# Dense steps of an input projection in runs of four, and a sum over values in one piece, in the interleaving of a decoder step

## The chip, the cores and the metric

The kernel runs on one core of one Trainium2 chip. The metric is the device time of a run in microseconds (us). The kernel before takes 839.37 us, the median of 3 runs (834.9 to 840.41).

## The reference

One step of a hybrid decoder layer, for a prompt of 512 tokens and for 8 sample sequences of 8 new tokens each behind 1024 past ones. Both groups go through the same weights, so the kernel treats them as 576 columns (T).

```python
h = _rmsnorm(x, norm1_w)
proj = h @ w_in                                   # 1024 -> 3584 columns, 28 tiles of 128
rq, rk, rv, rg, aq, ak, av = jnp.split(proj, points, axis=-1)
ro, ret_s = _retention(rq, rk, rv, ret_s0)        # 8 heads of 64, chunks of 128
ro = silu(rg) * group_norm(ro)
k_all = concat([win_k, ak]);  v_all = concat([win_v, av])
ao = _dilated_attention(aq, q_pos, k_all, v_all)  # 8 heads, softmax over three dilated windows
x = x + concat([ro, ao]) @ w_out
ua, ub = jnp.split(_rmsnorm(x, norm2_w) @ w_up, [D_FF])
x = x + (silu(causal_conv3(ua)) * ub) @ w_down    # D_FF = 2816
return _rmsnorm(x, normf_w), ...                  # and states, windows, conv rows
```

## The kernel before, in words

**Dense products.** The projections run in float32 exactness by splits: a weight tile (wraw, 128 x 1024) is split into whi (ACT, line 219) and wlo (DVE, line 229), the activations into a hi and a lo part as well. One *dense step* of k (line 254, in `dense`) is three passes (hi hi, lo hi, hi lo) over two halves of 288 columns, so six matmuls. A tile of 128 output columns takes 8 steps and sums into one of two big PSUM tiles (psd, the tile d). The weights come over SP's queue of DMAs in order of use.

**Two kinds of attention.** The heads go in four pairs (hp 0 to 3). Per pair the prompt has four *units* of 128 queries (`attn_unit`): a split of q (ACT, DVE line 755), scores (PE, 761 to 766), minimum (DVE, 773), exponential (ACT, 780), reciprocal (DVE, 783), scaling of the weights (POOL, 785), transposes (PE, 791), copies (ACT and DVE, 795), sums over values (PE, 804), and after the fourth a copy (ACT, 809). The sample group has two *units* per pair (`unit`), each of four sequences with 768 rows of the cache: per sequence two sets of three key transposes (PE, 877; six matmuls each in the trace since both sets stand together) with copies to kt (DVE and ACT, 878), then scores (PE, 887), minimum (DVE, 894), exponential (ACT, 899), reciprocal and scaling (DVE, 901 and 902), weight transposes (PE, 910 and 911), copies to spt (DVE and ACT, 914 to 916), sums over values (PE, 923; 28 groups), a copy ob (ACT, 932), its transpose (PE, 938) and the copies into aoT (DVE, 941). The cache tiles (kc, three buffers; vc, six) are loaded by SP ahead of their use. POOL copies the queries of a pair into a zero-padded tile (qb), one of which the sample scores need.

**Behind the products.** The 28 column tiles of the input projection (`in_proj`) each end in a scaling on DVE (526, 528), transposes of v and k to token order (PE, 495), or the gate (tile roT: SiLU on ACT, product on POOL, for the last pair on DVE, line 532). The tiles for attention of pair hp wait until six units of pair hp-2 are used. `mix_split` splits the attention and gate results (1009 and 1011) for the output projection, which is the next dense stage. Ahead of that stage SP issues the loads of the last norm's weights (nfw, 1285) and of the convolution state (csn, 1051); PE transposes csn in 22 tiny matmuls (1055).

**What sets the order.** Nothing is scheduled on the chip: each engine's queue is written at build time by `Merge` (lines 96 to 142). A *stream* is a generator that issues some instructions and yields (cost, latency): what its burst holds TensorE for, and how long the other engines then need before the stream's next burst can start. Streams with an amount of work left (the dense products of in_proj, and the parents of attention) advance in proportion to it; a stream without goes first as soon as it is ready. A dense step yields a cost of 738 ns. A stream that lacks something (a PSUM tile: four small ones, m, and the two big ones; a tile of another stream) yields None. Retention ends at `mg.run(lambda: fin_ret)`; from there to the output projection the streams are in_proj, the prompt units and the sample units.

```python
            ok = [e for e in free if e["at"] <= self.clock]
            if ok:
                e = min(ok, key=lambda e: (e["left"] is not None, e["vt"] if e["left"] else e["at"], e["n"]))
            else:
                e = min(free, key=lambda e: (e["at"], e["n"]))
                self.clock = e["at"]
```

Of the kernel before, what the change touches and what calls it, by code (L numbers as in the profile page):

```python
# [35 lines left out]
C0 = 224  # L36
# [59 lines left out]
class Merge:  # L96
    """Interleaves streams of tensor-engine work.

    A stream is a generator; it yields (cost, latency): what its last burst holds the tensor engine for,
    and how long the other engines then take before its next burst can start.  A third number, if given,  # L100
    takes the place of the cost in the pace.  None: it waits for another stream.  Streams with work
    left advance in proportion to it; a stream without goes first as soon as it is ready."""

    def __init__(self):
        self.clock, self.live, self.n = 0.0, [], 0

# [3 lines left out]
    def add(self, gen, left=None, delay=0.0):  # L110
        self.n += 1
        self.live.append({"g": gen, "left": left, "vt": self.floor(), "at": self.clock + delay, "n": self.n,
                          "stuck": False})

    def run(self, until=None):
        while self.live and not (until and until()):
# [3 lines left out]
            if ok:  # L120
# [9 lines left out]
            if c is None:  # L130
                e["stuck"] = True
                continue
            low = self.floor()
# [13 lines left out]
def decoder_step(ctx, tc, a):  # L147
# [14 lines left out]
    def room(n):  # L162
        """n of the small tiles of PSUM are free from here on; give() returns them when their readers are issued"""
# [13 lines left out]
    # ---- weights, streamed in order of use  # L177
# [67 lines left out]
    def dense(ps, key, xhi, xlo, k0, k1, first, last, rows=None, made=None):  # L245
        """ps[:, C0 + n] (+)= sum over k of w[k, cols]^T x[k, n], in three exact-split passes."""
# [19 lines left out]
    # ---- constants  # L266
# [31 lines left out]
    def rsqrt_steps(dst, v, t):  # L298
        """dst = v ** -0.5 for positive v: a seed from the exponent, then Newton's steps; t: scratch."""
# [24 lines left out]
    # ================= first norm  # L324
# [114 lines left out]
    def in_first():  # L439
        """the first two tiles of columns advance together as x arrives"""  # L440
# [34 lines left out]
    # ================= input projection, retention and dilated attention, by pairs of heads  # L475
# [13 lines left out]
    def natural(src, dst):  # L489
        """dst [token, tile, 128] = the transpose of src [128 features, T]"""  # L490
# [101 lines left out]
    # ---- retention  # L592
# [12 lines left out]
    def retention():  # L605
        for hp in range(4):
# [13 lines left out]
            # scores, transposed: [key, query]  # L620
# [19 lines left out]
            # states after each chunk  # L640
# [13 lines left out]
            # outputs  # L654
# [21 lines left out]
            # group norm; the decay of a row only scales its statistics  # L676
# [29 lines left out]
            # states of the sample group  # L706
# [616 lines left out]
```

## Time and profile before

| | before |
|---|---|
| median of 3 runs | 839.37 us (834.9 to 840.41) |
| profiled execution, span | 838.0 us, one execution |
| TensorE (PE) busy | 817.6 us, 98% |
| VectorE (DVE) busy | 414.1 us, 49% |
| ScalarE (ACT) busy | 295.2 us, 35% |
| GpSimd (POOL) busy | 148.4 us, 18% |
| from the end of retention to the output projection | 148.46 to 338.39 us of the span |
| DMA, mean over the span | 154 GB/s |

The profile is of one execution on the chip. PE is TensorE's matmuls, PEld its weight loads, SPq the queue of SyncE that issues DMAs; PEclk is the granted clock of TensorE as a share of full speed (1.00 is 2.4 GHz, 0.5 is 1.2 GHz). A row of a timeline names start, duration, engine, line, operation, out<-in with shapes, how many instructions it stands for, and in brackets the idle time ahead of it and what ended it. Matmuls are pipelined, so a row's duration overlaps the next; the distance from start to start is what a group costs.

### The profile page before, as it was taken

To read this page: it belongs to the slowest core of one execution; us is meant where nothing else is said; L and a number is where in the kernel's file an instruction comes from. 1 tells how busy PE (TensorE), PEld (TensorE's weight loads), DVE (VectorE), ACT (ScalarE), POOL (GpSimd) and SP (SyncE) were. 2 spreads that over 40 slices of the span, in tenths; PEclk is the share of its full clock that TensorE was granted. 3 is DMA by queue.
4 is the path that set the end of the run, shared out by engine and by line. 5 is a ranking of instruction groups with operands and counts; after the bars stand their busy time and mean duration, and the time that the engine had idled before them with its cause. 6 is when DMAs were issued, how large, how long until landed. Compare 5 with 4: busy or idle time off the path is not lost.

```text
span 838.0 us, 16048 instructions
## 1 busy us (share of the span) xinstructions
PE 817.6 (98%) x6594; PEld 775.0 (92%) x6594; DVE 414.1 (49%) x796; ACT 295.2 (35%) x511; POOL 148.4 (18%) x234
## 2 busy tenths in 40 slices
PE   7999999998999999999999999999999999999995
PEld 6999999886887888999999999999999999999995
DVE  5664655655556456544555455432235545545333
ACT  5322321544536367234223333311223323332222
POOL 1312111020111113022212222100012222210111
PEclk9999999999999999899999999999999999999999
DMA  9355562667796873555256544453334445553213
GB/s 268 104 167 163 162 201 70 184 187 217 201 251 184 237 201 85 109 176 169 84 179 198 176 158 138 135 170 87 94 101 156 146 152 176 170 169 81 70 51 114
DMA packets 179534, 128.68 MB, mean 154 GB/s; under 512 B 15425, under 2 KB 176101, under 8 KB 178914
## 3 DMA queue, kind: packets, MB, share of 16 engines
q1 hardware_dynamic: 178308, 93.75, 40.1%
q10 hardware_dynamic: 928, 33.63, 11.0%
q8 instruction: 52, 0.85, 0.4%
q0 software_dynamic: 224, 0.28, 0.1%
q14 instruction: 22, 0.18, 0.1%
HBM read 121.52 MB, written 39.66 MB: 192 GB/s over the span
## 4 chain that ended last, share of the span: by engine, by line
PE 92%; DMA 3%; DVE 1%; ACT 1%; SPq 1%; issue 1%; POOL 0%; ACTq 0%; DVEq 0%; POOLq 0%
PE d L254 72%; PE m L877 2%; PE d L451 2%; PE m L923 2%; DMA kc<-in_cache_win_k_dram 1%; PE m L791 1%; PE d L887 1%; PE m L495 1%; PE m L804 1%; PE px L410 1%; PE m L1213 1%; PE px L254 1%; DMA csn<-in_state_conv_dram 1%; PE m L663 1%; PE m L764 1%
## 5 line engine op out<-in xcount | busy, mean ns | idle before, releaser
L219 ACT ACTIVATE whi<-wraw 128x1024 fp32r<-128x1024 f32 (+2 forms) x114 | 110.8, 972 | 372.2 <-issue 182.1
L229 DVE TENSOR_TENSOR wlo<-wraw,whi 128x1024 fp32r<-128x1024 f32 (+2 forms) x114 | 126.8, 1112 | 119.8 <-ACT whi L219 116.8
L254 PE MATMUL d<-bhi,whi 128*128 128x288 f32 x768 | 174.6, 309 | 0.0
L254 PE MATMUL d<-bhi,wlo 128*128 128x288 f32 x768 | 165.0, 297 | 0.0
L254 PE MATMUL d<-blo,whi 128*128 128x288 f32 x768 | 164.8, 296 | 0.0
L254 PE MATMUL d<-hhi,whi 128*128 128x288 f32 x704 | 150.9, 296 | 0.0
L254 PE MATMUL d<-hlo,whi 128*128 128x288 f32 x704 | 150.8, 296 | 0.0
L254 PE MATMUL d<-hhi,wlo 128*128 128x288 f32 x704 | 150.7, 296 | 0.0
L254 PEld LDWEIGHTS d<-bhi,whi 128*128 128x128 f32 x768 | 122.4, 191 | 5.3 <-issue 3.6
L254 PEld LDWEIGHTS d<-bhi,wlo 128*128 128x128 f32 x768 | 124.1, 189 | 0.0
L254 PEld LDWEIGHTS d<-blo,whi 128*128 128x128 f32 x768 | 124.1, 190 | 0.0
L254 PEld LDWEIGHTS d<-hhi,whi 128*128 128x128 f32 x704 | 113.4, 189 | 0.1
L254 PEld LDWEIGHTS d<-hhi,wlo 128*128 128x128 f32 x704 | 113.4, 189 | 0.0
L254 PEld LDWEIGHTS d<-hlo,whi 128*128 128x128 f32 x704 | 113.4, 189 | 0.0
L1122 DVE TENSOR_TENSOR ue<-d,rstd_b 128x512 f32<-128x512 f32 x22 | 15.2, 691 | 74.5 <-PE d L254 74.5
L1141 POOL TENSOR_TENSOR g<-g,cv 128x512 f32<-128x512 f32 x20 | 25.8, 1290 | 142.5 <-DVE g L1138 137.1
L785 POOL TENSOR_SCALAR s<-s,sc 128x128 f32<-128x128 f32 (+3 forms) x32 | 18.2, 578 | 141.7 <-DVE sc L783 140.4
L1038 POOL TENSOR_TENSOR acc<-acc,sq 128x576 f32<-128x576 f32 x13 | 21.4, 1646 | 111.5 <-ACT sq L1037 111.5
L1127 POOL COPY cout<-ue 128x2 f32<-128x2 f32 x22 | 5.7, 259 | 137.6 <-DVE ue L1122 137.6
L877 PE MATMUL m<-ident,kc 128*128 128x128 f32 x192 | 27.5, 277 | 2.1 <-DMA kc<-in_cache_win_k_dram 2.1
L878 DVE COPY kt<-m 128x384 f32<-128x384 f32 x32 | 17.8, 556 | 23.2 <-PE m L877 22.6
L878 ACT COPY kt<-m 128x384 f32<-128x384 f32 x32 | 15.3, 477 | 38.5 <-PE m L877 38.0
(261 smaller groups left out, 1033.7 us busy)
## 6 DMA issues: line engine op xcount, KB each, us to landing
wraw<-in_w_up_dram SPq DMA_DIRECT2D x44, 512.0 KB
wraw<-in_w_in_dram SPq DMA_DIRECT2D x26, 512.0 KB
kc<-in_cache_win_k_dram SPq DMA_DIRECT2D x32, 256.0 KB
vc<-in_cache_win_v_dram SPq DMA_DIRECT2D x32, 256.0 KB
wraw<-in_w_down_dram SPq DMA_DIRECT2D x16, 384.0 KB
wraw<-in_w_down_dram SPq DMA_DIRECT2D x16, 320.0 KB
kc<-in_cache_win_k_dram SPq DMA_DIRECT2D x64, 64.0 KB
vc<-in_cache_win_v_dram SPq DMA_DIRECT2D x64, 64.0 KB
```

The source lines that it names most:

```text
L219: act.activation(split[i][0][:, c], raw[i][:, c], AF.Copy)
L229: dve.tensor_sub(lo[:, c], raw[i][:, c], f32(hi[:, c]))
L254: pe.matmul(ps[:, C0 + s * H2:C0 + (s + 1) * H2], wt[:, rows[k] if rows else k - k0], x[k][:, s * H2:(s + 1) * H2], start=first and k == k ...
L410: pe.transpose(ps[:, s], xn[:r, j, k * P:(k + 1) * P], ident[:r, :r])
L451: pe.matmul(ps[i][:, C0 + s * H2:C0 + (s + 1) * H2], wt[:, k], x[k][:, s * H2:(s + 1) * H2], start=k == 0 and wt is hi and x is xhis, stop ...
L785: pool.tensor_scalar(s[:, :n], s[:, :n], c[:, 2:3], 1.0, op0=OP.mult, op1=OP.mult)
L877: pe.transpose(ps[:, j * P:(j + 1) * P], K[u, x][:, 3 * w + j], ident)
L878: (act.copy if w else dve.tensor_copy)(kt[:, w * 384:w * 384 + 384], ps[:, :384])
L923: pe.matmul(ps[x * 32:(x + 1) * 32, :P], pt[:n, j, x * 32:(x + 1) * 32], v, start=j == 0, stop=j == 6, tile_position=(0, x * 32))
L1038: pool.tensor_tensor(acc, acc, sq, op=OP.add)
L1122: dve.tensor_mul(u[:, 2:NP + 2], ya[:, :NP], rstd_b[:, :NP])
L1141: eng.tensor_tensor(g[:, :NP], g[:, :NP], c[:, :NP], op=OP.mult)
```

## The change

`Merge` gets a number `keep` (1, as before, or 4) and remembers which stream ran last and how many bursts in a row it has run. A stream that was added as dense, that ran last and is still ready goes on until it has run `keep` bursts. Only in_proj is added as dense; keep is 4 from the end of retention to the end of `mix_split`. In the sample unit the sums over values no longer hand back after the fourth of seven row blocks. Comments and docstrings also went, so that a line of before stands 8 lines further on after it in the functions named above (L254 is L262, L923 is L931).

```diff
     def __init__(self):
         self.clock, self.live, self.n = 0.0, [], 0
+        self.keep, self.burst, self.last = 1, 0, None
...
-    def add(self, gen, left=None, delay=0.0):
+    def add(self, gen, left=None, delay=0.0, dense=False):
...
             ok = [e for e in free if e["at"] <= self.clock]
-            if ok:
+            if self.last in ok and self.burst < self.keep:
+                e = self.last
+            elif ok:
                 e = min(ok, key=lambda e: (e["left"] is not None, e["vt"] if e["left"] else e["at"], e["n"]))
...
             if c is None:
                 e["stuck"] = True
+                if e is self.last:
+                    self.last = None
                 continue
+            self.burst = self.burst + 1 if e is self.last else 1
+            self.last = e if e["dense"] and c[0] and e in self.live else None
...
                     pe.matmul(ps[x * 32:(x + 1) * 32, :P], pt[:n, j, x * 32:(x + 1) * 32], v, start=j == 0, stop=j == 6,
                               tile_position=(0, x * 32))
-                if j == 3:
-                    yield 900.0, 0.0
             for x in range(4):
                 del V[u, x]
-            yield 800.0, 600.0
+            yield 1700.0, 600.0
...
-    mg.add(in_proj(), 130.0e3)
+    mg.add(in_proj(), 130.0e3, dense=True)
...
     mg.run(lambda: fin_ret)
     rpx.close()
+    mg.keep = 4
...
     mg.add(mix_split())
     mg.run()
+    mg.keep = 1
```

What this does to the order of the queues stands at three places. First TensorE in the middle of the stage, around the transpose of the first sample unit's result (tile ob; qa and ql are the splits of q of a prompt unit, s its weights, n the values of a pair in token order). Before, from the sums over values on:

```order
L923 MATMUL m<-vc,spt 32x128 x8
L923 MATMUL m<-n_1727,spt 32x128 x4
L764 MATMUL m<-kdec,qa_2061 128x512
L764 MATMUL m<-ka_1767,qa_2062 128x512
L766 MATMUL m<-kdec,ql 128x512
L766 MATMUL m<-ka_1767,ql 128x512
L254 MATMUL d<-bhi,whi 128x288 x2
L254 MATMUL d<-blo,whi 128x288 x2
L254 MATMUL d<-bhi,wlo 128x288 x2
L877 MATMUL m<-ident,kc 128x128 x6
L938 MATMUL m<-ident,ob 128x128
L254 MATMUL d<-bhi,whi 128x288 x2
```

And now, from the same scores of 512 columns on:

```order
L774 MATMUL m<-kdec,ql 128x512
L774 MATMUL m<-ka_1810,ql 128x512
L812 MATMUL m<-pt,n_1747 64x128 x6
L944 MATMUL m<-ident,ob 128x128
L885 MATMUL m<-ident,kc 128x128 x6
L769 MATMUL m<-t_1807,t_1952 128x128 x2
L895 MATMUL d<-kt,qb_404 32x512 x4
L895 MATMUL d<-kt,qb_404 32x264 x4
L799 MATMUL m<-ident,s 128x128 x10
L885 MATMUL m<-ident,kc 128x128 x6
L812 MATMUL m<-pt,n_2127 64x128 x2
L812 MATMUL m<-pt,n_1747 64x128 x8
```

The dense steps that stood between the scores, the transposes and the scores of the next unit are gone from here; the next of them comes behind the second sample unit's sums over values.

Second, TensorE at the end of the stage, from the last unit but one on. Before:

```order
L791 MATMUL m<-ident,s 128x128 x8
L923 MATMUL m<-vc,spt 32x128 x24
L923 MATMUL m<-n_3797,spt 32x128 x4
L254 MATMUL d<-bhi,whi 128x288 x2
L254 MATMUL d<-blo,whi 128x288 x2
L254 MATMUL d<-bhi,wlo 128x288 x2
L804 MATMUL m<-pt,n_3797 64x128 x8
L254 MATMUL d<-bhi,whi 128x288 x2
```

Now the dense steps of the input projection are all done ahead of this:

```order
L799 MATMUL m<-ident,s 128x128 x8
L931 MATMUL m<-vc,spt 32x128 x24
L931 MATMUL m<-n_3689,spt 32x128 x4
L812 MATMUL m<-pt,n_3689 64x128 x8
L885 MATMUL m<-ident,kc 128x128 x6
L944 MATMUL m<-ident,ob 128x128
L895 MATMUL d<-kt,qb_406 32x512 x4
L895 MATMUL d<-kt,qb_406 32x264 x4
L918 MATMUL d<-ident,ss 128x128 x6
L919 MATMUL d<-ident,ss 64x128
L931 MATMUL m<-vc,spt 32x128 x24
L931 MATMUL m<-n_3689,spt 32x128 x4
```

The last sample unit's scores, weight transposes and sums follow each other, where dense steps stood between all of them.

Third, VectorE at the same end, around the split of q (ql) for the last prompt unit. Before, with a scaling of the input projection (t) and a split of weights (wlo) ahead of it:

```order
L894 ISA ss,ssc<-d,sb 128x776
L894 ISA ssc 128x1
L526 TENSOR_TENSOR t_4173<-d,rstd_b 128x576
L795 COPY pt<-m 128x384
L229 TENSOR_TENSOR wlo<-wraw,whi 128x1024
L755 TENSOR_TENSOR ql<-t_3590,qa_4157 64x128
L755 TENSOR_TENSOR ql<-t_3590,qa_4158 64x128
```

And now, with the reciprocals of the unit before it (sc) ahead, and the last gate product (roT) behind:

```order
L886 COPY kt<-m 128x384
L902 ISA ss,ssc<-d,sb 128x776
L902 ISA ssc 128x1
L791 RECIPROCAL sc<-sc 128x1 x2
L763 TENSOR_TENSOR ql<-t_3466,qa_4148 64x128
L763 TENSOR_TENSOR ql<-t_3466,qa_4149 64x128
L540 TENSOR_TENSOR roT<-roT,t_4105 128x576
L781 ISA s,sc<-m,pb 128x512
```

The split of q now stands behind reciprocals, which come after exponentials on ACT; and the product of the last gate tile, which was the last work of the stage on VectorE, stands before the last prompt unit's minimum.

## Rows read from the trace of the kernel before

**Rows 1.** The page, part 1: busy us, share of the span, instructions.

```profile
PE 817.6 (98%) x6594; PEld 775.0 (92%) x6594; DVE 414.1 (49%) x796; ACT 295.2 (35%) x511; POOL 148.4 (18%) x234
```

**Rows 2.** Windows: start:end, length, busy (instructions) of each engine, clock, DMA share, GB/s.

```profile
148.46:338.39 189.93, 185.52 (x1815) 156.23 (x1815) 109.31 (x281) 102.80 (x247) 29.86 (x73) 1.00 0.69 193
192.85:202.42 9.57, 7.20 (x95) 5.37 (x93) 5.30 (x14) 4.96 (x14) 0.89 (x4) 1.00 0.88 250
338.39:347.34 8.95, 8.95 (x68) 8.72 (x66) 7.67 (x11) 4.17 (x6) 0.47 (x2) 1.00 0.50 97
347.34:350.98 3.64, 2.15 (x24) 2.11 (x23) 0.00 (x0) 0.00 (x0) 0.00 (x0) 0.77 1.20 252
350.98:356.30 5.32, 5.32 (x23) 5.32 (x23) 1.33 (x2) 0.00 (x0) 0.00 (x0) 0.52 0.39 95
```

**Rows 3.** Timeline of PE, the stretch without dense steps.

```profile
192.85 0.82 PE L877 MATMUL m<-ident,kc 128*128 128x128 f32 x6
...
196.13 0.89 PE L877 MATMUL m<-ident,kc 128*128 128x128 f32 x6 [1.15 <-DMA kc<-in_cache_win_k_dram]
197.40 1.00 PE L761 MATMUL m<-t,t 64*128 64x128 f32 x4 [0.39 <-DVE kt L878]
198.33 1.52 PE L923 MATMUL m<-vc,spt 128*32 128x128 f32 x48
...
200.13 1.10 PE L877 MATMUL m<-ident,kc 128*128 128x128 f32 x6
201.95 0.71 PE L791 MATMUL m<-ident,s 128*128 128x128 f32 x2 [0.72 <-POOL s L785]
```

**Rows 4.** Timeline of PE, just before that stretch.

```profile
187.25 1.51 PE L887 MATMUL d<-kt,qb 128*32 128x512 f32 x16
188.69 1.09 PE L804 MATMUL m<-pt,n 128*64 128x128 f32 x16
189.72 0.53 PE L254 MATMUL d<-bhi,whi 128*128 128x288 f32 x2
...
190.61 0.82 PE L877 MATMUL m<-ident,kc 128*128 128x128 f32 x6
191.19 0.51 PE L254 MATMUL d<-bhi,whi 128*128 128x288 f32 x2
...
192.06 0.43 PE L254 MATMUL d<-bhi,whi 128*128 128x288 f32 x2
```

**Rows 5.** Groups by line and form, end of retention to output projection: busy, mean ns | idle before.

```profile
L780 ACT ACTIVATE s<-s,sc 128x512 f32<-128x512 f32 x8 | 5.7, 714 | 1.0 <-DVE sc L773 0.9
L785 POOL TENSOR_SCALAR s<-s,sc 128x512 f32<-128x512 f32 x8 | 5.5, 697 | 30.4 <-DVE sc L783 30.4
L780 ACT ACT_TABLE_LOAD x2 | 2.6, 1283 | 0.0
```

**Rows 6.** Timeline of DVE and of ACT, one sample unit from minimum to scaling.

```profile
188.91 0.97 DVE L894 CUSTOM_DVE_ANT_0 ss<-d,sb 128x776 f32<-128x776 f32 x1 [1.65 <-PE d L887]
190.32 0.95 ACT L899 ACTIVATE ss<-ss,ssc 128x776 f32<-128x776 f32 x1
191.62 0.16 DVE L901 RECIPROCAL ssc<-ssc 128x1 f32<-128x1 f32 x1
191.81 0.62 DVE L902 TENSOR_SCALAR ss<-ss,ssc 128x776 f32<-128x776 f32 x1
```

**Rows 7.** SP from 300 to 352 us: a wait (total, times, longest), and an issue.

```profile
SPq L1285 <- DVE roT L532: 20.8, 1, 20.8
...
342.44 0.38 SPq L1051 DMA_DIRECT2D csn<-in_state_conv_dram  x1
```

**Rows 8.** Timeline of PE where the conv state arrives, in the output projection.

```profile
348.84 2.21 PE L1055 MATMUL m<-ident,csn 16*128 16x16 f32 x22 [1.50 <-DMA csn<-in_state_conv_dram]
...
351.62 0.68 PE L254 MATMUL d<-blo,whi 128*128 128x288 f32 x2
352.10 0.68 PE L254 MATMUL d<-bhi,wlo 128*128 128x288 f32 x2
```

## What the change does to the time: the prediction

> **What bounds the kernel now.** I read the page first, then the windows of the stretch that the change reorders, then its timeline on TensorE, then the waits. The page has TensorE (PE) busy for 98% of the span [rows 1], so a microsecond is won or lost where PE stands still or turns slowly. The change acts from the end of retention, at 148.5 us of the span, to the first step of the output projection, at 338.4 us. In those 189.93 us PE is busy for 185.52 [rows 2]: 4.4 us of gaps, all clock at 1.00. This stage mixes two kinds of work. Dense steps (six matmuls, all on weights that are there) can run at any time. Attention groups come in chains: scores on PE, minimum on DVE, exponential on ACT, reciprocal on DVE, scaling on POOL or DVE, transposes on PE, copies on ACT and DVE, sums over values on PE. Each group waits for other engines, and the dense steps between them are what hides the waits. So the reader should look for the one place where before has no dense steps: from 192.85 to 202.42 [rows 3]. There the queue waits 1.15 us for a cache tile, 0.39 for a copy and 0.72 for POOL. Windows give 7.20 us busy of 9.57 there [rows 2].
>
> **The change, part by part.** *Fewer switches.* The order has 118 dense steps in this stretch before and after, in 67 runs before and 29 after. A step that follows other work takes 0.87 us (191.19 to 192.06) or 0.89 (189.72 to 190.61); one that follows a dense step takes 0.79 (192.06 to 192.85) [rows 3, 4]. So 38 entries fewer at 0.08 to 0.10 each: 3.0 to 3.8, taken as **-3.2 us**. The one-piece sum over values removes no matmul; only three of the eight units were cut in before's order, and its gain is inside the 38.
>
> *Waits that lose their cover.* The kept dense stream spends its steps early. It may not run more than two pairs of heads ahead (its tile of hp waits until the units of hp-2 are used), and it ends before attention does. The new order has three stretches without a dense step: the first from the scores of pair 0's third prompt unit on, with two whole sample units in it; the second when pair 1 ends and pair 2 begins; the third at the end, up to the output projection. I added their PE groups at their quickest turns, start to next start (six key transposes 0.58, a unit's sample scores 1.44, its value sums 1.80, the largest prompt value sums 1.03 [rows 3, 4], the other kinds between 0.1 and 1.1 likewise): 21.0, 13.8 and 17.1 us, 51.9 in all. In before only the stretch of [rows 3] has this form.
>
> How long PE waits in them I worked out twice. *By the yardstick:* the dense-free stretch of before has 2.37 us idle per 7.20 busy, 0.33; but groups in it also wait inside (a set of key transposes takes 1.27 from 196.13 to 197.40, not 0.58), and at quickest turns its work is 5.6 of 9.57, so 0.71. On 51.9 us that is **17 to 37 us**. *By walking the queues* of the after order with durations of the trace:
> First stretch, 9.6 us. Transposes of weights and keys wait for small PSUM tiles whose copies stand behind score minima on DVE and copies on ACT: 2.6. Scores of the last prompt unit and the next pair, same cause: 1.2. The second sample unit's scores need the new keys that POOL copies in; POOL stands before them at two 512-wide scalings (0.70 each) that wait for two exponentials (0.71 each) [rows 5]: 2.2. The next 256-wide scores need a split of q on DVE, behind the sample unit's scaling (0.62 [rows 6]): 1.5. Its transposes come 2.1 before their chain is done.
> Second stretch, 5.8 us: 3.0 for the first unit of pair 2, whose chain minimum, exponential, reciprocal, scaling has only sample scores and one set of transposes to hide it; 0.95 for a copy of sums that stands on ACT behind key copies; 1.9 for small ones.
> Third stretch, 11.6 us. The split of q for the last prompt unit stands on DVE behind reciprocals, these wait for 384-wide exponentials, and those on ACT behind four casts and a table load of 1.28 us [rows 5]: PE is done with the groups ahead at about 5 us and gets the split at 9.5: 4.7. Transposes and value sums of the unit before it: 1.9. The last sample unit has nothing beside it at all: from the end of its scores (188.69 in the unit shown) come the minimum 0.97, exponential 0.95, reciprocal 0.16 and scaling 0.62 [rows 4, 6], 2.7 us and four hand-overs, 3.2 in all; then 0.65 for the copies ahead of its value sums, 0.45 for the one behind them; 0.7 for small ones.
> Together **+27 us**, in the middle of the yardstick's bounds. The walk has no contention in it, the upper end has; the lower end counts gaps alone. I keep 17 and 37 for the range. Against it, the 4.4 us of gaps of before go away or are counted in the walk: **-4.4**.
>
> *Behind the stage.* The load of the conv state (csn) is third in a row of waits on SP: the norm weights ahead of it wait 20.8 us for the product of the last gate tile [rows 7]. In before this tile is the last work of the stage; csn lands at 348.84, PE waits 1.5 us for it after the first 11 steps of the output projection, and behind that gap and 22 tiny transposes the clock is at 0.50, 1.2 GHz: pairs of matmuls at 0.48 us (351.62 to 352.10) instead of 0.27 [rows 2, 8]. That is 11 pairs, 5.32 us instead of 2.9. After the change the gate tile ends some 20 us ahead of the output projection, csn waits only for the last value sums, and the same 11 dense steps (8.8 us) cover it; in before it took 6.4 us from issue (342.44 [rows 7]) to landing. Gain 1.5 + 2.4 = **-3.9 us**, zero if csn is late or the clock falls all the same.
>
> Moved on SP and DVE: the cache loads keep their order; in the dense-free stretches they are asked for faster. Before moves 193 GB/s over the stage and 250 in its dense-free stretch [rows 2]; a set of key and value tiles is 0.77 MB, 3.1 us at that rate, and the second stretch wants six in 19 us with three loaded ahead: 9 us, covered. Cost nothing; if the cover is gone, some 3 us per late set. Splits of weights on ACT and DVE come in pairs ahead of a run of four steps (3.2 us); one split of each fits. Nothing.
>
> *Clock.* At 195 to 202 us PE stood for 1.15, 0.39 and 0.72 us and the windows keep 1.00 [rows 2, 3]; after the 1.5 us and the tiny transposes at 347 it fell [rows 2, 8]. The new waits are 2 to 5 us long. I put nothing into the sum, 2.4 us per fall into the range. The Trainium skill (TensorE: Matmul & The Clock Gate, Why this matters for your kernels) says that idle gaps between bursts of matmuls put the clock back to half; that would make the three stretches cost about 7 us more, and the rows at 347 agree with it, those at 195 show gaps that were too short.
>
> **Sum.** -3.2 - 4.4 + 27 - 3.9 = +15.5. The profiled span of 838.0 becomes 853.5; the median of the runs is 1.4 above the span, so **855 us**.
>
> **Rivals.** *All covered, faster.* If the chains run as well without dense steps as with them, the three stretches keep only the 4.4 us that before has, and what stays is 3.2 + 3.9: 832 us, or 828 if those 4.4 go as well. For it: DVE is busy for 109 and ACT for 103 of the 190 us, so neither is full. Against it: [rows 3], where the same chains without dense steps left PE waiting for a third to two thirds of its work. The point from which it decides: below 11.5 us of waits the change gains.
> *Short waits, no change.* The walk may overrate queues: 12 to 20 us of waits give 840 to 848. For it: small latencies that I took in line can overlap.
> *Clock falls or cache tiles late, slower still.* Half clock behind each stretch, or a late set of tiles in two of them: 7 us more, 862; with the upper yardstick 868 and above. For it: two waits of the third stretch are each longer than the one at 347. Against it: most gaps stand between full groups of matmuls.
> That the change does not do what it says is no rival: the order shows the runs of four.
>
> **How the numbers follow.** Forecast, 20 to 37 us of waits and no fall, 848 to 865: 0.52. Short waits, 840 to 848: 0.22. Clock or tiles, 860 to 875: 0.12. All covered, 829 to 838: 0.14. A measurement can tell about 1% here, 8.4 us: slower than 847.8 is the first and the third, 0.64; within 1% the second and 0.06 of the last, 0.28; faster than 831, 0.08. The range from 840 (12 us of waits) to 868 (37 us and one fall) leaves out 0.14 below and 0.05 above.
>
> **What would show it.** Right: dense steps at 0.87 after other work, but 29 entries; three stretches in which PE waits for POOL's key copies, DVE's splits and ACT's exponentials, 27 us in sum, the longest before the last prompt unit's scores and the last sample unit's transposes; no wait for csn, no 0.50 clock behind it. Wrong: PE's waits in these stretches below 12 us; or waits for cache tiles as the main releaser; or the clock at 0.50 there; or a stage (148.5 us to the output projection) that is shorter than 190 us, where I expect 190 + 27 - 4.4 - 3.2 = 209.

## The result, and the profile after

The changed kernel takes 875.75 us, the median of 6 runs (874.25 to 878.69), where the kernel before takes 839.21 beside it (834.9 to 841.45, 6 runs). The ratio is 1.0449, with a 95% interval from 1.0427 to 1.0471: 36.5 us slower. The prediction had the sign, at 855 us, but the time lies above its range of 840 to 868.

The page of after has 874.8 us of span and puts less of it into work. Its first part (busy us, share of the span, instructions) answers to [rows 1]:

```profile
PE 832.2 (95%) x6594; PEld 784.7 (90%) x6594; DVE 413.5 (47%) x796; ACT 298.1 (34%) x513; POOL 145.8 (17%) x234
```

The same 6594 matmuls are busy 14.6 us longer, and 22.2 us more of the span are idle. The windows say where (start:end, length, busy us of each engine, clock, DMA share, GB/s). The first line is the whole stage, from the end of retention to the output projection; the next three are the stretches without dense steps; the last is the output projection up to the conv state:

```profile
149.01:377.99 228.98, 200.98 (x1814) 166.61 (x1814) 107.93 (x277) 104.35 (x248) 28.06 (x75) 0.93 0.58 162
183.71:220.12 36.41, 28.93 (x279) 19.49 (x277) 19.54 (x64) 19.32 (x59) 6.41 (x18) 0.91 0.53 154
247.77:268.96 21.19, 17.71 (x224) 13.02 (x224) 12.57 (x42) 12.11 (x36) 3.38 (x10) 0.92 0.56 164
343.28:377.99 34.71, 26.03 (x249) 17.46 (x248) 15.20 (x40) 14.11 (x34) 3.20 (x10) 0.76 0.29 87
377.99:388.60 10.61, 10.61 (x67) 10.46 (x67) 8.31 (x13) 4.33 (x6) 0.00 (x0) 0.83 0.52 115
```

The stage grew from 189.93 us [rows 2] to 228.98, by 39.05. It holds 28.0 us without a matmul (228.98 - 200.98) where before held 4.4, and its matmuls take 200.98 us where they took 185.52: the clock is 0.93 in the mean where it was 1.00. The three stretches have 7.5, 3.5 and 8.7 us of idle time, 19.7 in sum; so 8.3 us of it lie outside them, where the prediction had put none. Behind the stage 2.8 us came back: the 11 steps of the output projection run at 0.83, but nothing waits for csn.

What PE waited for (engine, line <- releaser: us in total, times, longest):

```profile
PE d L918 <- DVE sc L791: 3.9, 1, 3.9
PE m L799 <- POOL s L793: 3.8, 3, 2.3
PE m L774 <- DVE ql L763: 3.4, 2, 2.6
PE d L918 <- DVE ss L910: 3.0, 1, 3.0
PE d L895 <- DVE t L564: 2.3, 1, 2.3
PE d L895 <- POOL kt L983: 2.1, 1, 2.1
PE d L262 <- DVE ssc L902: 1.8, 2, 1.4
```

The second, third, fourth and sixth are waits that the prediction named, in the stretches. The first, fifth and seventh are not. They stand at places outside the stretches, and they are all on d, the two big PSUM tiles. The first and the fifth have one cause, which the rows below show. The seventh is another: there a dense step waits for a big tile that a sample unit's scores had filled (ssc is the output of the minimum that empties it). The timeline around the first of them, on PE (start, length, engine, line, operation, shapes, count, idle time ahead of it):

```profile
322.94 0.43 PE L262 MATMUL d<-bhi,whi 128*128 128x288 f32 x2
323.21 0.42 PE L262 MATMUL d<-blo,whi 128*128 128x288 f32 x2
...
327.76 1.51 PE L918 MATMUL d<-ident,ss 128*128 128x128 f32 x6 [3.86 <-DVE sc L791]
...
329.14 0.83 PE L262 MATMUL d<-bhi,whi 128*128 128x288 f32 x2
329.77 0.68 PE L262 MATMUL d<-blo,whi 128*128 128x288 f32 x2
330.25 0.55 PE L262 MATMUL d<-bhi,wlo 128*128 128x288 f32 x2
```

and on ACT and DVE in the same microseconds:

```profile
324.63 1.06 ACT L227 ACTIVATE whi<-wraw 128x1024 fp32r<-128x1024 f32 x1
325.72 1.23 DVE L237 TENSOR_TENSOR wlo<-wraw,whi 128x1024 fp32r<-128x1024 f32 x1 [4.66 <-ACT whi L227]
326.86 0.75 DVE L534 TENSOR_TENSOR t<-d,rstd_b 128x576 f32<-128x576 f32 x1
```

A column tile of the input projection was finished before 320.5. The scaling that empties it (L534) starts at 326.86, because it stands on DVE behind a split of weights (wlo) for a *later* tile; that split waits for whi, and whi stands on ACT behind exponentials and casts. With one tile still full and the next one being filled, the sample unit's weight transposes have no big tile and wait 3.86 us for one. The releaser in brackets (sc L791, a reciprocal) is merely the DVE instruction issued behind the scaling. Behind the wait the pairs of matmuls are 0.48 us apart (329.77 to 330.25), where they were 0.27 ahead of it (322.94 to 323.21): half clock.

### The profile page after: what moved, and what is told of

It reads as the page before. It is cut to its first block, busy times and chain, and to the rows that moved or that the text cites. A ratio compares the mean times of both kernels' runs of the same rounds, so it can differ in the third digit from the quotient of the medians.

```text
span 874.8 us, 16063 instructions
## 1 busy us (share of the span) xinstructions
PE 832.2 (95%) x6594; PEld 784.7 (90%) x6594; DVE 413.5 (47%) x796; ACT 298.1 (34%) x513; POOL 145.8 (17%) x234
## 4 chain that ended last, share of the span: by engine, by line
PE 91%; ACT 3%; DVE 3%; DMA 1%; issue 1%; SPq 0%; POOL 0%; ACTq 0%; DVEq 0%; POOLq 0%
PE d L262 70%; PE m L885 3%; PE m L931 2%; PE d L459 2%; PE d L895 1%; PE m L812 1%; PE m L799 1%; PE m L503 1%; PE d L918 1%; PE m L1221 1%; PE px L418 1%; PE px L262 1%; PE m L671 1%; PE m L774 1%; DMA vrows<-in_norm_w_dram 1%
## 5 line engine op out<-in xcount | busy, mean ns | idle before, releaser
L262 PE MATMUL d<-bhi,whi 128*128 128x288 f32 x768 | 171.3, 305 | 1.8 <-DVE ssc L902 1.8
L262 PE MATMUL d<-bhi,wlo 128*128 128x288 f32 x768 | 165.0, 296 | 0.0
L262 PE MATMUL d<-blo,whi 128*128 128x288 f32 x768 | 164.8, 296 | 0.0
L262 PE MATMUL d<-hhi,whi 128*128 128x288 f32 x704 | 151.0, 296 | 0.0
L262 PE MATMUL d<-hhi,wlo 128*128 128x288 f32 x704 | 150.7, 296 | 0.0
L262 PE MATMUL d<-hlo,whi 128*128 128x288 f32 x704 | 150.7, 296 | 0.0
L262 PEld LDWEIGHTS d<-bhi,whi 128*128 128x128 f32 x768 | 123.2, 190 | 4.8 <-issue 2.6
L262 PEld LDWEIGHTS d<-blo,whi 128*128 128x128 f32 x768 | 124.2, 190 | 0.0
L262 PEld LDWEIGHTS d<-bhi,wlo 128*128 128x128 f32 x768 | 124.1, 189 | 0.0
L262 PEld LDWEIGHTS d<-hhi,whi 128*128 128x128 f32 x704 | 113.4, 189 | 0.1
L262 PEld LDWEIGHTS d<-hhi,wlo 128*128 128x128 f32 x704 | 113.4, 189 | 0.0
L262 PEld LDWEIGHTS d<-hlo,whi 128*128 128x128 f32 x704 | 113.4, 189 | 0.0
L1046 POOL TENSOR_TENSOR acc<-acc,sq 128x576 f32<-128x576 f32 x13 | 21.2, 1631 | 113.3 <-ACT sq L1045 113.3
L885 PE MATMUL m<-ident,kc 128*128 128x128 f32 x192 | 30.1, 297 | 0.3 <-ACT pt L803 0.2
```

Source lines behind the costliest of these rows:

```text
L262: pe.matmul(ps[:, C0 + s * H2:C0 + (s + 1) * H2], wt[:, rows[k] if rows else k - k0], x[k][:, s * H2:(s + 1) * H2], start=first and k == k ...
L885: pe.transpose(ps[:, j * P:(j + 1) * P], K[u, x][:, 3 * w + j], ident)
L1046: pool.tensor_tensor(acc, acc, sq, op=OP.add)
```

## The experiments

Four theories. **Stretches**: the loss is waits for chains of attention in the stretches without dense steps, as forecast, only longer. **Late emptying**: with the kept stream, the scaling that empties a finished tile is written after the next tile's first four steps, so behind the split of weights that the second of these steps issues. Before, the stream handed back after one step and the scaling came ahead of the split. **Half clock**: the gaps put the clock down, and the matmuls behind them cost the rest. **One piece**: the undivided sum over values costs time by itself.

How the scaling and the split stood on DVE before, in one such place:

```profile
229.91 0.74 DVE L556 SCALAR_TENSOR_TENSOR t<-d,rstd_b 128x576 f32<-128x576 f32 x1
230.78 1.23 DVE L229 TENSOR_TENSOR wlo<-wraw,whi 128x1024 fp32r<-128x1024 f32 x1
```

All times in one table; each ratio is to the kernel before, run beside it on the same chip. Where the text gives a difference by the ratios as well, that is the fairer one, since the kernel before differed by up to 2 us between the groups of runs.

| kernel | median us | ratio, 95% interval |
|---|---|---|
| changed kernel | 875.75 | 1.0449, 1.0427 to 1.0471 |
| one_piece_alone | 841.75 | 1.0039, 1.0021 to 1.0058 |
| evacuate_first | 878.75 | 1.0461, 1.0429 to 1.0493 |
| filled_waits | 872.78 | 1.0402, 1.0371 to 1.0434 |
| fours_in_the_middle | 857.76 | 1.0218, 1.0192 to 1.0245 |
| fours_alone | 867.7 | 1.0353, 1.0318 to 1.0388 |
| first_stretch | 857.37 | 1.0227, 1.0175 to 1.0280 |
| two_stretches | 859.28 | 1.0254, 1.0201 to 1.0307 |
| runs_of_two | 864.62 | 1.0309, 1.0271 to 1.0347 |
| split_later | 868.38 | 1.0329, 1.0283 to 1.0374 |
| all_filled | 871.67 | 1.0376, 1.0343 to 1.0409 |
| conv_state_first | 835.76 | 0.9967, 0.9942 to 0.9991 |
| other_pace | 841.11 | 1.0013, 0.9994 to 1.0032 |
| later_fours_alone | 866.85 | 1.0356, 1.0318 to 1.0393 |
| later_runs_of_two | 849.83 | 1.0147, 1.0123 to 1.0171 |
| later_fours_in_the_middle | 849.85 | 1.0150, 1.0125 to 1.0174 |
| later_and_filled | 859.52 | 1.0256, 1.0235 to 1.0277 |

### The two parts apart

**one_piece_alone**: the second half of the change without the first.

```diff
-    mg.keep = 4
+    mg.keep = 1
```

> Edit: keep stays 1, only the sums over values in one piece (the second half of the change alone). Theory 'runs of four' (the whole loss of 36 us comes from the kept dense stream): the order keeps 65 runs of dense steps and no stretch without them, so the time is that of the kernel before, 837 to 842 us. Rival 'one piece' (the undivided sum delays the groups behind it by up to 0.9 us in each of eight units): up to 7 us more, 843 to 847.

Measured: 841.75 us, 0.39% above before, some 3 us. Nearly all of the loss belongs to the runs of four.

**other_pace**: a control. An order that differs from before in many places, without runs of four.

```diff
-    mg.add(in_proj(), 130.0e3)
+    mg.add(in_proj(), 132.0e3)
```

> Edit: the kernel before with one number of the planner's pace changed, 132 us of dense work instead of 130, as a control: the order of pairs 1 and 2 differs in many places, keep stays 1, no stretch without dense steps is longer than before's. Theory 'order matters only where cover is missing': within 2 us of the kernel before, 836 to 841. Rival 'any order but the tuned one costs some us' (which would also be the 3 us of the sum in one piece by itself): 841 to 848.

Measured: 841.11 us, ratio 1.0013, which is no difference that this measurement can tell. One other order, then, costs nothing that can be told; runs of four do.

**fours_alone**: the first half without the second.

```diff
+                if j == 3:
+                    yield 900.0, 0.0
             for x in range(4):
                 del V[u, x]
-            yield 1700.0, 600.0
+            yield 800.0, 600.0
```

> Edit: the changed kernel with the sums over values in two pieces again (keep 4 alone). Theory 'runs of four': 872 to 878 us, that of the changed kernel less at most the 3 us that the one piece cost by itself. Rival 'the two parts need each other' (a sum in two pieces lets other groups in between where dense steps are gone): 862 to 870.

Measured: 867.7 us, 8 less than the changed kernel. This is the rival's number (862 to 870), not the theory's. Its waits have no 3.9 us ahead of weight transposes, for in this order no sample unit meets a full tile at that place. later_fours_alone, below, returns to this.

### One stretch, two stretches

**first_stretch** and **two_stretches**: keep falls back to 1 when 6, or 12, units of attention are used. Up to there the orders are those of the changed kernel.

```diff
-        used[hp] = used.get(hp, 0) + 1
+        used[hp] = used.get(hp, 0) + 1; mg.keep = 4 if sum(used.values()) < 6 else 1
```

> Edit: the changed kernel, but keep goes back to 1 when six units of attention are used. The order is word for word that of the changed kernel up to the end of its first stretch without dense steps (18.7 us of TensorE work at quickest turns), and has no second or third one. Theory 'waste lies in the stretches' (in the changed kernel's trace the first takes 36.4 us for 18.7 of work, the wait before it 2.3 with some 1.7 of half clock behind it): 17.7 + 4 over the 841.8 of keep 1 with the sum in one piece, less 2 or 3 of gaps that the old order had there: 858 to 862 us. Rival 'loss grows with the number of runs of four' (8 of 27): 850 to 853.

> Edit: the changed kernel, but keep goes back to 1 when twelve units are used: the first and the second stretch without dense steps stay as they are, the third is gone. Theory 'waste lies in the stretches' (the second takes 21.2 us for 13.5 of work): 7 to 9 us over the kernel with the first stretch alone, 866 to 870. Rival 'by the number of runs' (13 of 27): 856 to 860.

Measured: 857.37 and 859.28 us. The first stretch, with the run-up to it, costs 2.27% - 0.39%, about 16 us, close to what the first theory gave. The second costs hardly anything more (2 us, with intervals that overlap), where the theory had 7 to 9. The third with what stands ahead of it makes the rest, 4.49% - 2.54%, about 16 us. So the loss does not grow with the number of runs, and it is not in proportion to the work in the stretches either.

**runs_of_two**: keep 2.

```diff
-    mg.keep = 4
+    mg.keep = 2
```

> Edit: the changed kernel with keep at 2. The order has 40 runs and two stretches without dense steps in the middle, 9.9 and 8.6 us of TensorE work at quickest turns, none at the end. Theory 'waste lies in the stretches' (40.4 us of waste for 51.9 of work in the changed kernel, 0.78 per us): 0.78 x 18.5 = 14 over the 841.8 of keep 1, 852 to 858. Rival 'runs by themselves' (a run of two holds the chains a third as long as one of four, 1 step instead of 3): 841.8 + 12 = 854, the same; so this run fixes the size and does not tell them apart, its trace does: by the first, the waits stand in the two stretches; by the second they are spread.

**fours_in_the_middle**: runs of four, but no long stretch without dense steps.

```diff
-        used[hp] = used.get(hp, 0) + 1
+        used[hp] = used.get(hp, 0) + 1; mg.keep = 4 if 12 <= sum(used.values()) < 16 else 1
```

> Edit: the changed kernel, but keep is 4 only while 12 to 15 units of attention are used, and 1 before and after. The order has eleven runs of four or more in the middle and no stretch without dense steps longer than 5 us of work. Theory 'stretches without dense steps': runs of four cost little as long as dense steps are left between the chains: 839 to 845 us (late emptying of big tiles in it, up to 4). Rival 'each run of four delays the chains by itself' (36 us over 27 runs): 12 us or more, 851 to 855.

Measured: 864.62 and 857.76 us, both more than the theory of stretches allows. Among their longest waits are waits for big tiles whose scaling (t) is late: 3.7, 2.9 and 1.3 us in the one, 4.2 us in the other. The theory of stretches alone fell with these two. The lines of runs_of_two:

```profile
PE d L262 <- DVE t L534: 3.7, 1, 3.7
PE d L895 <- DVE t L534: 2.9, 1, 2.9
PE d L895 <- DVE t L570: 1.3, 1, 1.3
```

### Late emptying

**evacuate_first** lets the dense stream hand back to the planner after a finished tile.

```diff
             mg.add(in_post(m, ps))
+            if mg.keep > 1:
+                yield 0.0, 0.0
```

> Edit: the changed kernel, but in_proj hands back once, at no cost, after it has finished a column tile, so that the scaling that empties the tile is issued ahead of the next tile's steps and of its split of weights on DVE. Theory 'late emptying' (with keep 4 the scaling that empties a big PSUM tile is written four steps later, behind a split of weights, and scores and weight transposes wait for that tile: 2.3 us at 172.6, 0.5 at 230.4, 1.4 at 312.2, 3.9 at 327.8, 8.0 in sum, with some 3.4 us of half clock behind the two longer ones): 8 to 11 us less than the changed kernel, 864 to 868; those waits are gone, the waits of the three stretches without dense steps stay. Rival 'only the three stretches matter' (what waits there would wait in another place): 873 to 877.

Measured: 878.75 us, no gain, against an expected 864 to 868. The two waits for late scalings are gone from its trace. But the edit changes a yield, so the planner wrote a different order for TensorE too: its three stretches without dense steps take 38.4, 23.1 and 41.7 us, where those of the changed kernel take 36.4, 21.2 and 34.7. So this run says nothing on the tile alone. **split_later** lets the scaling come ahead of the split without touching TensorE's queue (the load of weights behind the split also moves, by one step):

```diff
+            late = 3 if key[0] == "in" and mg.keep > 1 else 0
-            if k == k0 + 1:
+            if k == k0 + 1 + late:
                 w_split_lo(i + 1)
-            if k == k0 + 3:
+            if k == k0 + 3 + late // 3:
                 w_load(i + 4)
```

> Edit: the changed kernel, but from the end of retention on, the split of the next tile's weights on DVE (wlo) and the load behind it are issued three steps later, so that the scaling that empties a finished big PSUM tile stands ahead of the split on DVE instead of behind it. TensorE's order is word for word that of the changed kernel. Theory 'late emptying costs time of its own' (waits of 2.3 us at 172.6 and 3.9 us at 327.8 with half clock behind both, and 0.4 and 1.8 at the starts of dense tiles): 6 to 10 us less, 866 to 870. Rival 'chains of attention set the time of these places, the tile is only the last thing waited for': 873 to 877, with waits of about the same length put down to other releasers.

Measured: 868.38 us, 7.4 less than the changed kernel (by the ratios 1.2%, 10 us; their intervals leave some 4 us either way). The stage is 223.60 us long where it was 228.98. Its first four waits are forecast ones, and those for t L564 and sc L791 are gone. The fifth, for the tile of a sample unit's scores, stayed as it was; it has nothing to do with the split:

```profile
150.81:374.41 223.60, 200.44 (x1815) 166.19 (x1814) 109.61 (x277) 104.05 (x248) 30.08 (x75) 0.92 0.59 166
```

```profile
PE m L800 <- POOL s L794: 4.4, 4, 2.3
PE m L775 <- DVE ql L764: 3.4, 2, 2.6
PE d L919 <- DVE ss L911: 3.0, 1, 3.0
PE d L896 <- POOL kt L984: 2.1, 1, 2.1
PE d L262 <- DVE ssc L903: 1.8, 2, 1.4
```

The same edit on three of the other kernels, TensorE's order unchanged in each:

> Edit: keep 2 (as runs_of_two, 864.6 us) with the split of weights three steps later, TensorE's order unchanged. Theory 'late emptying': the waits of 1.3, 3.7 and 2.9 us for scalings of finished tiles (at 296, 308 and 326) go: 6 to 9 us less, 856 to 859. Rival 'other work is waited for there': 862 to 866.

> Edit: keep 4 in the middle only (as fours_in_the_middle, 857.8 us) with the split of weights three steps later for tiles begun while keep is 4, TensorE's order unchanged. Theory 'late emptying': of its loss the wait of 4.2 us at 269.9 with 1.5 to 4 of half clock behind it goes: 851 to 855; the rest is waits of chains, 4.3 us at the last sample unit among them. Rival 'runs of four delay the chains and the tile is only what is seen': 856 to 860.

> Edit: keep 4 with the sums over values in two pieces (as fours_alone, 867.7 us), and the split of weights on DVE three steps later (as split_later). TensorE's order is that of fours_alone. Theory 'late emptying': fours_alone has one such wait, 2.3 us at 172.0, and not the 3.9 us at 327.8 of the changed kernel: 1 to 4 us less, 864 to 867; with split_later at 868.4 the sum in one piece then costs 2 to 4 us, as it did with keep 1 (2.9). Rival 'the sum in one piece costs 8 us beside runs of four': 858 to 861.

Measured: 849.83 us for runs of two (14.8 less, by the ratios 1.62% or 13.6 us, about twice what was expected), 849.85 for fours in the middle (7.9 less, by the ratios 0.68% or 5.7 us), 866.85 for fours alone (0.9 less, ratios the same). Late emptying is so about half of the 3.09% that runs of two lost, and about a third of the 2.18% that fours in the middle lost. It cannot be told from nothing in fours alone, where the trace shows one wait of 2.3 us for a tile. With late emptying out of the way, the sum in one piece makes no difference that can be told (868.38 and 866.85): its 8 us beside runs of four were a tile that was emptied late.

The mechanism in fours_in_the_middle, first on DVE, then PE's first dense step behind it:

```profile
272.22 1.23 DVE L237 TENSOR_TENSOR wlo<-wraw,whi 128x1024 fp32r<-128x1024 f32 x1 [3.02 <-ACT whi L227]
273.36 0.75 DVE L564 SCALAR_TENSOR_TENSOR t<-d,rstd_b 128x576 f32<-128x576 f32 x1
```

```profile
274.16 0.85 PE L262 MATMUL d<-bhi,whi 128*128 128x288 f32 x2 [4.24 <-DVE t L564]
```

and the same in later_fours_in_the_middle, where the scaling no longer waits for a split:

```profile
268.77 0.75 DVE L565 SCALAR_TENSOR_TENSOR t<-d,rstd_b 128x576 f32<-128x576 f32 x1
...
271.91 1.22 DVE L237 TENSOR_TENSOR wlo<-wraw,whi 128x1024 fp32r<-128x1024 f32 x1 [0.88 <-ACT whi L227]
```

```profile
269.58 0.52 PE L263 MATMUL d<-bhi,whi 128*128 128x288 f32 x2
```

The scaling starts at 268.77 instead of 273.36, and the 4.24 us are gone.

### Half clock

**filled_waits** puts matmuls, the results of which are thrown away, ahead of groups for which PE waits, and **all_filled** more of them.

```diff
+    def fill(dst, n, c0=0, c1=256):
+        for _ in range(n):
+            pe.matmul(dst[:, c0:c1], xhi[:, 7, 0:P], xhi[:, 7, P:P + c1 - c0], start=True, stop=True)
...
             ps = dtile()
+            if u == 7:
+                fill(ps, 24)
             for j in range(6):
```

> Edit: the changed kernel with matmuls whose results are thrown away (256 or 224 columns, on tiles that are there) ahead of five groups for which PE waited: 18 of them before the second half of the scores of sample unit 1 (waited 2.1 us), 10 before the transposes of prompt unit 1 of pair 1 (1.3), 18 before those of unit 0 of pair 2 (2.3), 30 before the last prompt unit's scores (3.7), 24 before the weight transposes of the last sample unit (3.0). The rest of the work is the changed kernel's. Theory 'the gaps put the clock down' (15.5 us of PE's added busy time is half clock behind waits): nothing that PE waited for comes earlier, but behind these five the clock stays at 1.00, which is worth 10 to 14 us: 861 to 866 us. Rival 'half clock has another cause, or costs nothing since the chains on the other engines set the time': 873 to 880.

> Edit: as filled_waits, with thrown-away matmuls also ahead of the first sample unit's scores (19), the weight transposes of sample unit 6 (32, both into a small tile of their own), its last value sums (5) and some shorter waits (3 to 12 each). Theory 'half clock costs its whole amount' (clock 0.976 over the span against 0.994 with keep 1, 16 us): 860 to 863. Rival 'half clock mostly takes the place of waits' (filled_waits raised the clock to 0.987, which is 9.6 us of clock, and gained 3 to 4): another 1 to 4 us less than filled_waits, 868 to 872.

Measured: 872.78 us at a clock of 0.987, and 871.67 at 0.994 (0.976 without). That is 3 and 4 us (by the ratios 4 and 6) of the 16 that the clock seemed to cost, about the rivals' numbers. One set in all_filled stood in the wrong place, though: the wait of 3.9 us was that of sample unit 5, and the 32 matmuls ahead of unit 6 (3.9 us) were work that hid nothing. The clean form is **later_and_filled**, which fills on top of split_later and leaves that set out:

> Edit: split_later (868.4 us, clock 0.977) with thrown-away matmuls ahead of ten groups of the stretches without dense steps, as all_filled has them but without the two sets in small tiles of their own (one of those stood ahead of a unit that had not waited, so that all_filled held up to 3.8 us of matmuls too many). Theory 'half clock costs part of its amount': 3 to 6 us less, 862 to 866. Rival 'its whole amount' (0.017 of 868, 15 us): 852 to 855. What is then left over the kernel before is waits for chains at full clock.

Measured: 859.52 us at a clock of 0.997, 8.9 less than split_later (by the ratios 0.73%, 6 us, again with some 4 us either way). That lies between the numbers of the theory (862 to 866) and of its rival (852 to 855). Apart from the thrown-away matmuls it keeps TensorE's order of the changed kernel. Its stage:

```profile
148.65:361.18 212.53, 203.51 (x1943) 172.69 (x1943) 109.19 (x277) 104.03 (x248) 30.00 (x75) 1.00 0.61 175
```

So holding the clock was worth 6 to 9 us, a third to a half of the 17 us that the clock alone would make ((0.997 - 0.977) x 868). The likely reason, which no run isolates, is that where the other engines set the time, slower matmuls take the place of waiting; thrown-away matmuls that ran longer than the wait would also make the gain smaller. What is left over before, 2.56% or 21 us, is at full clock, so by elimination waits of chains.

### Behind the stage

**conv_state_first**: the kernel before, with csn loaded ahead of nfw.

```diff
         sp.dma_start(csn[:16], a["state_conv"].rearrange("b j f -> (b j) f"))
+        sp.dma_start(nfw, bass.AP(tensor=a["normf_w"].tensor, offset=a["normf_w"].offset, ap=[[0, P], [1, D]]))
...
-    sp.dma_start(nfw, bass.AP(tensor=a["normf_w"].tensor, offset=a["normf_w"].offset, ap=[[0, P], [1, D]]))
     mg.add(conv_state_in(), None)
```

> Edit: the kernel before, with the load of the conv state (csn) issued ahead of that of the last norm's weights (nfw), so that it no longer stands behind the wait of 20.8 us for the last gate tile. Theory of the prediction's term behind the stage: csn lands before the first 11 steps of the output projection end, PE's wait of 1.5 us goes and with it the half clock behind the 22 tiny transposes, 3.9 us: 834.5 to 836. Rival 'the tiny transposes put the clock down by themselves': only 1.5 us, 837 to 838; or csn waits for its own memory until the last value sums and lands late all the same: 838 to 840.

Measured: 835.76 us, 0.33% faster than before (0.09 to 0.58%), about 3 us, and faster than both kernels. The load goes out at 333.40 instead of 342.44 [rows 7], on SP:

```profile
333.40 0.33 SPq L1051 DMA_DIRECT2D csn<-in_state_conv_dram  x1
```

and on PE the tiny transposes follow the dense steps without a wait and run in 1.5 us, where [rows 8] had 2.2 behind a wait of 1.5; the window behind them has the clock at 1.00:

```profile
347.05 1.53 PE L1056 MATMUL m<-ident,csn 16*128 16x16 f32 x22
```

```profile
348.51:353.00 4.49, 4.49 (x36) 4.49 (x35) 1.53 (x3) 0.43 (x1) 0.00 (x0) 1.00 0.43 112
```

So the half clock of [rows 2] did not come from the transposes by themselves. Whether the wait alone would have brought it, no run shows.

## Why the prediction went wrong

**The direction, and the waits that lose their cover: right.** The sum had +27 us for waits in three stretches, and the stage at 209 us. The trace of after shows 19.7 us of idle time there, beside matmuls that run at half clock. With the two effects out of the way that the sum had not priced, the changed order has a stage of 212.53 us (later_and_filled). The places were right too. The wait for POOL's key copies was 2.1 us (2.2 forecast), that ahead of the last sample unit's weight transposes 3.0 (3.2), that ahead of the last prompt unit's scores 2.6 and 1.1 (4.7):

```profile
349.12 0.51 PE L772 MATMUL m<-kdec,qa 128*128 128x512 f32 x1 [1.07 <-ACT qa L760]
...
352.86 0.79 PE L774 MATMUL m<-kdec,ql 64*128 64x512 f32 x1 [2.62 <-DVE ql L763]
...
371.70 1.54 PE L918 MATMUL d<-ident,ss 128*128 128x128 f32 x6 [2.99 <-DVE ss L910]
```

**"One split of each fits. Nothing": the step that failed.** The prediction counted what a split of weights costs on ACT and DVE, and found room for it. It did not ask what stands behind the split on DVE. With runs of four that is the scaling that empties the finished tile, and for its tile wait the scores and weight transposes of the sample units and the next dense tile. What queues behind an instruction was named for reciprocals and exponentials in the stretches, not for the instructions that the dense stream itself issues. Moving the split later took 7 to 10 us off (split_later), the half clock behind these two waits included.

**"Clock: I put nothing into the sum": the second step that failed.** [rows 3] showed gaps of 1.15 us and less at 1.00, and the prediction knew that the new waits would be 2 to 5 us long. It kept the clock for a rival at 0.12, at 2.4 us per fall. In the trace of after it falls behind each of the six waits of 2 us or more; in the third stretch it is 0.76 in the mean. The prediction had named a clock of 0.50 in the stretches as a sign that it was wrong, and the sign came. With late emptying out of the way, holding the clock took another 6 to 9 us off (later_and_filled). The rule of the Trainium skill (TensorE: Matmul & The Clock Gate, Why this matters for your kernels) that the prediction weighed, that idle gaps between bursts of matmuls put the clock back to half, agrees with the trace of after. The prediction's 7 us for it lie within what was measured, in part by luck: they stood for one fall in each of three stretches, and the trace has two in the first and two in the third.

**The term behind the stage: right.** The forecast was -3.9 us; conv_state_first gives about 3 (0.09 to 0.58%), and after has no wait for csn. Half clock still reached the output projection, from the last sample unit's waits: its first 11 steps took 10.61 us, where [rows 2] has 8.95.

**The sum in one piece: small, but a loss.** The prediction put it inside a gain; by itself it costs 0.39%, some 3 us. What it does in the changed kernel cannot be told from nothing once tiles are emptied in time.

**The sum again.** The forecast 15.5, 7 to 10 for late emptying, 6 to 9 for half clock and up to 3 for the sum in one piece make 29 to 38 us; measured were 36.5. The two prices each have some 4 us of uncertainty either way, so this shows only that no large term is missing. The 3.2 us for fewer switches could not be seen by themselves: no run has the runs of four without their waits.

Still open: why the second stretch costs almost nothing in two_stretches, though it shows 3.5 us of idle time and a clock of 0.92 in the changed kernel.

## What to carry to other kernels

When a stream of work that hides waits is made to run in longer bursts, ask not only where it will be missing, but also which of its own clean-up instructions now come later, and behind what they stand in their queue: here a scaling that frees one of two PSUM tiles fell behind a split of weights. To test such a thing, move the instruction in its own engine's queue and leave TensorE's order alone; an edit that a planner sees changes everything at once. Waits between groups of matmuls that are longer than the ones seen at full clock are to be priced with the half clock behind them; here that came to a third to a half of its nominal cost.

## What the runs showed of the hardware

The granted clock stayed at 1.00 through gaps of 1.15, 0.39 and 0.72 us within ten [rows 2, 3]. In after it was between 0.50 and 0.69 behind waits of 2.1 to 3.9 us. Windows of 4 us at the six, in the columns as above:

```profile
172.00:176.00 4.00, 3.41 (x23) 2.05 (x24) 0.58 (x2) 0.00 (x0) 0.84 (x4) 0.69 0.91 236
200.00:204.00 4.00, 3.68 (x18) 2.48 (x18) 1.97 (x9) 1.64 (x6) 1.39 (x7) 0.60 0.57 167
258.00:262.00 4.00, 3.12 (x14) 2.51 (x16) 2.69 (x11) 3.22 (x11) 0.78 (x2) 0.60 0.62 177
328.00:332.00 4.00, 4.00 (x24) 3.96 (x24) 0.92 (x2) 0.97 (x3) 1.98 (x3) 0.69 1.07 292
352.00:356.00 4.00, 2.48 (x7) 1.36 (x8) 3.56 (x10) 1.71 (x5) 1.17 (x2) 0.50 0.51 150
372.00:376.00 4.00, 3.35 (x43) 2.77 (x45) 0.56 (x1) 0.63 (x2) 0.00 (x0) 0.50 0.02 6
```

The length of a single wait does not settle it. In the first stretch the clock fell once more, from 211 on, behind waits of 0.57, 0.39 and 0.80 us between 205 and 210.2; a wait of 1.36 us that ended at 312.19, with dense steps behind it, left it at 1.00:

```profile
211.00:215.00 4.00, 2.72 (x14) 2.28 (x13) 1.55 (x8) 2.29 (x8) 0.53 (x2) 0.57 0.58 161
312.00:316.00 4.00, 3.81 (x30) 3.84 (x30) 2.81 (x6) 2.89 (x5) 0.00 (x0) 1.00 0.71 218
```

Matmuls of no use, put ahead of the groups that wait, held it at 1.00 through the whole stage (later_and_filled), and that was worth 6 to 9 us although their results are thrown away.
